# A decoder layer on one core: moving tiles at another residue of 512 bytes, and a re-ordered opening of the FFN

## The chip, the cores and the metric

The kernel runs on one core of a Trainium2 chip. The metric is the device time of one execution in microseconds (us); lower is better. The engines are named as in the profile: PE is the matrix engine (PEld its weight loads), DVE the vector engine, ACT the scalar engine, POOL the general-purpose one, SP the queue that issues most transfers.

## The reference

One layer of a hybrid decoder, 512 tokens by 1024 features, fp32, depth 1. Two token mixers read the same input projection; their outputs are gated, merged and projected; then comes a SwiGLU channel mixer (FFN) with 2816 hidden features.

```python
proj = h @ w_in                        # q_a k_a v_a r_a d_low q_b k_b v_b g_a g_b
y_a = (norm(gla(q_a, k_a, v_a, decay(d_low))) * silu(r_a)) @ w_branch_a
y_b = swa(rope(q_b), rope(k_b), v_b, sinks) @ w_branch_b
mix = (sigmoid(g_a) * y_a + sigmoid(g_b) * y_b) @ w_out
h = layer_norm(alpha * h + mix, ln1_g, ln1_b)
ffn = (silu(h @ w_gate) * (h @ w_up)) @ w_down
h = layer_norm(alpha * h + ffn, ln2_g, ln2_b)
```

## The kernel before

**Products.** Every operand of a large product is split into a high part, rounded to fp32r (`ACT.copy`, the tiles `..h`), and a low part, the remainder (a DVE subtraction, the tiles `..l`); a product is the three matmuls high·high, low·high, high·low. A matmul streams its *moving* operand, 128 partitions by 512 or 256 columns of 4 bytes, past a *stationary* operand of 128x128 that a weight load has put into the array. In the profile `pga<-xh,wh` reads: into `pga`, moving `xh`, stationary `wh`. There are two families. In `feat_tile` (L239) activations move and weights stand still: `pq`, `pka`, `pqa`, `pr`, `pgb`, `pga` stream x (`xh`, `xl`), `pbb` and `pba` stream the two mixers' outputs. In `pva` (L435), in the output projection `pw` (L793 and L802) and in the down projection `pdn` (L1059) weights move and activations stand still.

**Stages in order of time.** Input projection with both mixers woven into it; `pbb`, `pga`, `pba`; the output projection, columns 0 to 511 first (`pw0` to `pw3`, L793), then columns 512 to 1023 one token tile at a time (`out_half`, `pw1_0` to `pw1_3`, L802); LayerNorm and the FFN's first operands; the FFN's gate and up products; the down projection in two column halves (`pdn0`, `pdn1`); the last LayerNorm.

**The FFN** is a Strassen-Winograd scheme: for each of 11 column groups `i` the 2x2 block product is made of seven products (`seventh`, L918, 256 columns each) of sums of weight quarters (`b11`, `b12`, `b22`, `b21`; the sums `t1` = b11+b12, `t2` = b11+b22, `t3` = b12+b22, `t4` = b11+b21, each a DVE addition of 128x1024 in place, `weight_sum`, L896) with sums of activation quarters (`A11`, `A12`, `A22`, `S1` to `S4`). `prep_quarters(n)` makes sure that the first n weight operands are split (`whb`/`wlb` from plain quarters, `wht`/`wlt` from sums; L905 on ACT, L906 on DVE). `A11` and `A12` come from the normalised rows: for token tile t the sum `res` (`norm_part`, L739: one DVE scalar_tensor_tensor on the PSUM tile, then bn_stats), the statistics' root (`ya`, `wa`), the normalisation of both halves on ACT (L753), four transposes for each half on PE (`pt_h`, L823), the affine step on ACT (`h`, L841), and the split (`a`, L830/L831).

**Order and memory.** The program is written stage by stage, and a scheduler sets the order of instructions on each engine from its own estimates; `tc.issue_after(ins)` makes it place what is inside behind `ins`. Tiles come from pools; the left stack of pools (weights, scratch, late tiles, FFN tiles) and the right one (x parts, merged activations, sums) grow toward each other, and a tile's address is fixed by what was allocated before it. Three small fillers shift whole stacks: `LEVEL` (left), `EDGE` (right), `BESIDE` (between FFN operands). So a residue of a tile's address modulo 512 bytes is the same for a whole family. `piece(j, k)` makes the down projection's stationary operand `op` from the activation `act`, from a ring of n buffers.

Of the kernel before, what the change touches and what calls it, by code (L numbers as in the profile page):

```python
# [9 lines left out]
F32 = mybir.dt.float32  # L10
# [3 lines left out]
ALU = mybir.AluOpType  # L14
AX = mybir.AxisListType

P = 128
# [10 lines left out]
ALPHA = 2.0 ** 0.25  # L28
# [4 lines left out]

LEVEL, EDGE, BESIDE = 32, 24, 16

C_QA, C_KA, C_VA, C_RA, C_DL = 0, 512, 1024, 2048, 3072
C_QB, C_KB, C_GA, C_GB = 3088, 4112, 4368, 5392
# [3 lines left out]
def tile_decoder_layer(  # L43
# [23 lines left out]
    PE, ACT, DVE, POOL = nc.tensor, nc.scalar, nc.vector, nc.gpsimd  # L67

    const = ctx.enter_context(tc.tile_pool(name="const", bufs=1))
    small = ctx.enter_context(tc.tile_pool(name="small", bufs=6))  # L70
    level = ctx.enter_context(tc.tile_pool(name="level", bufs=1))
    level.tile([P, LEVEL], F32, tag="level", name="level")
    wpool = ctx.enter_context(tc.tile_pool(name="weights", bufs=1))
    psum = ctx.enter_context(tc.tile_pool(name="psum", bufs=4, space=bass.MemoryType.PSUM))

# [7 lines left out]
    right = phase("xparts", "right")  # L83
# [652 lines left out]
    def norm_part(ps, t, i, stats, slot, c0=0, c1=512, first=True):  # L736
        r = res[t][i][:, c0:c1]
        if first:
            DVE.scalar_tensor_tensor(r, r, ALPHA, ps[:, c0:c1], ALU.mult, ALU.add)  # L739
        else:  # L740
            DVE.tensor_tensor(r, r, ps[:, c0:c1], ALU.add)
        DVE.bn_stats(stats[:, slot, :], r)

    def norm_rows(t, stats, name):
        mv = stat(f"mv{name}{t}", 2)
# [50 lines left out]
    def out_half(t):  # L796
        ps = ps_mm(f"pw1_{t}")
        ts = slice(t * P, (t + 1) * P)
        n = 0
        for k in range(NK):  # L800
            for d, w in ((mh, wo[k][0]), (ml, wo[k][0]), (mh, wo[k][1])):
                PE.matmul(ps, d[k][:, ts], w, start=n == 0, stop=n == 3 * NK - 1)  # L802
                n += 1
        norm_part(ps, t, 1, st1[t], 1)

# [90 lines left out]
    def prep_quarters(count):  # L898
        while len(parts_) < min(count, len(flow)):
            j = len(parts_)  # L900
            i, q = flow[j]
            weight_sum(i, q)
            src = raw_pair(i)[SUMS[q][0] if q in SUMS else q]
            wh, wl = [wpool.tile([P, 1024], F32R, tag=t, name=f"{t}{q}{i}", bufs=5) for t in ("wh", "wl")]
            ACT.copy(wh, src)  # L905
            lows.append(DVE.tensor_tensor(wl, src, wh.bitcast(F32), ALU.subtract))  # L906
            parts_.append((wh, wl))
            if i > 1 and j + 1 < len(flow) and flow[j + 1][0] == i:
                weight_sum(*flow[j + 1])
            if q == "t1" and 0 < i < HF - 1:  # L910
                raw_pair(i + 1)
# [65 lines left out]
            acts[h, i] = act_tile(h, i)  # L977
            DVE.tensor_tensor(acts[h, i], g, u, ALU.mult)

    prep_quarters(4)  # L980
    for t in range(NT):
        norm_part(pw[t], t, 0, st1[t], 0)
    for i in (0, 1):
        weight_sum(i, "t1")
    for t in range(NT):
        out_half(t)
        norm_rows(t, st1[t][:, 0:2, :], "a")
        if 1 <= t <= 2:
            first_tokens(t - 1)
    right.release()  # L990
    right = phase("sums", "right")
    A22, S4 = [operand(right, n) for n in ("a22", "s4")]
    right.tile([P, BESIDE], F32, tag="beside", name="beside2")
    right2 = phase("sums2", "right")
    S1, S2, S3 = [operand(right2, n) for n in ("s1", "s2", "s3")]
    h22, s1, s3 = plain("h22"), plain("s1f"), plain("s3f")
# [29 lines left out]

    def piece(j, k):
        if (j, k) not in pieces:
            home, n = (tail, 8) if j else (right2, 6)
            op = home.tile([P, 2, T], F32R, tag="op", name=f"op{j}_{k}", bufs=n)  # L1030
            if not pieces:
                right2.tile([P, BESIDE], F32, tag="beside", name="beside3")
            src = acts[k // HF, k % HF]
            ACT.copy(op[:, 0], src)  # L1034
            DVE.tensor_tensor(op[:, 1], src, op[:, 0].bitcast(F32), ALU.subtract)  # L1035
            pieces[j, k] = op
        return pieces[j, k]
# [92 lines left out]
```

## Time and profile before

| what | value |
|---|---|
| time, three runs | 865.37, 869.77, 870.14 us (median 869.77) |
| the profiled execution | 870.17 us, of which the span from first to last instruction is 868.2 us |
| mean granted PE clock | 0.995 |
| PE / DVE / ACT / POOL busy | 97% / 67% / 46% / 11% of the span |
| transfers | 83.13 MB, mean 96 GB/s |

The profile is one execution. "Mean of one" in a group of matmuls is the modelled length of one matmul, which overlaps its neighbours; what a matmul takes in a stream is the spacing of starts, which is the length of a stretch in which PE never pauses, divided by the number of matmuls that start in it (a window's count also includes those that reach in over an edge).

### The profile page before, as it was taken

The numbers are of one execution on the slowest core, as the hardware profiler recorded it, in microseconds if no ns is written. First come the engines' busy times: TensorE is split into PE (matmuls) and PEld (weight loads), VectorE is DVE, ScalarE is ACT, GpSimd is POOL, SyncE is SP. The second block draws the span as 40 slices with busy tenths as digits, with TensorE's granted clock in tenths as the row PEclk, the third lists the DMA queues.
The fourth block names the chain that finished last, engine by engine and source line by source line (L and its number), as shares of the span: only waits on it lengthen the run. The fifth ranks groups of instructions, "written<-read, shape, count | busy, mean of one in ns | idle before, by whom it ended". The sixth has DMA issues, their size and how long they took to land.

```text
span 868.2 us, 12541 instructions
## 1 busy us (share of the span) xinstructions
PE 841.2 (97%) x4922; PEld 726.7 (84%) x4922; DVE 578.0 (67%) x997; ACT 401.2 (46%) x699; POOL 94.5 (11%) x102
## 2 busy tenths in 40 slices
PE   7999999999999999999999898999999999999995
PEld 7887777787888788888888788999999999888884
DVE  4898888586675623322444669987878786964447
ACT  4557565564453422122233295554545455642321
POOL 4240220021320131000123000000000000000001
PEclk9999999999999999999999999999999999999998
DMA  8423113113113223333328301244333326242202
GB/s 243 145 74 95 52 49 98 49 49 98 49 49 97 73 74 97 97 97 97 97 97 263 101 1 46 77 143 130 113 102 99 97 73 209 84 145 92 79 1 97
DMA packets 92683, 83.13 MB, mean 96 GB/s; under 512 B 4833, under 2 KB 79601, under 8 KB 92625
## 3 DMA queue, kind: packets, MB, share of 16 engines
q1 hardware_dynamic: 90480, 76.89, 29.2%
q0 software_dynamic: 1568, 4.41, 1.6%
q10 hardware_dynamic: 576, 1.05, 0.3%
q8 instruction: 38, 0.62, 0.3%
q14 instruction: 21, 0.16, 0.1%
HBM read 80.24 MB, written 2.10 MB: 95 GB/s over the span
## 4 chain that ended last, share of the span: by engine, by line
PE 91%; DVE 3%; SPq 2%; DMA 1%; issue 1%; ACT 1%; POOL 0%; POOLq 0%; DVEq 0%; ACTq 0%
PE pdn L1059 13%; PE fx L918 13%; PE fy L918 7%; PE pva L435 5%; PE pgb L239 5%; PE pq L239 5%; PE pga L239 5%; PE pr L239 5%; PE pbb L239 5%; PE pba L239 5%; PE fz L918 4%; PE pka L239 3%; PE pqa L239 3%; PE pw L802 3%; PE po L416 2%; PE pp L405 2%
## 5 line engine op out<-in xcount | busy, mean ns | idle before, releaser
L171 DVE TENSOR_TENSOR wl<-raw,wh 128x1024 fp32r<-128x1024 f32 x96 | 121.3, 1265 | 111.7 <-ACT wh L170 111.5
L170 ACT CAST wh<-raw 128x1024 fp32r<-128x1024 f32 x96 | 100.5, 1050 | 133.5 <-PE pdn L1059 34.3
L1059 PE MATMUL pdn<-wh,op 128*128 128x512 f32 (+1 forms) x396 | 110.7, 366 | 0.0
L1059 PEld LDWEIGHTS pdn<-wh,op 128*128 128x128 f32 x396 | 71.4, 189 | 12.2
L905 ACT CAST wht<-b 128x1024 fp32r<-128x1024 f32 x44 | 46.2, 1049 | 63.9 <-DVE b L896 52.9
L1059 PE MATMUL pdn<-wl,op 128*128 128x512 f32 (+1 forms) x198 | 72.0, 365 | 0.0
L918 PE MATMUL fx<-s,wht 128*128 128x256 f32 x352 | 63.4, 280 | 1.4 <-ACT wht L905 1.4
L906 DVE TENSOR_TENSOR wlt<-b,wht 128x1024 fp32r<-128x1024 f32 x44 | 53.7, 1222 | 9.9 <-ACT wht L905 9.9
L896 DVE TENSOR_TENSOR b<-b,b 128x1024 f32<-128x1024 f32 x44 | 53.5, 1220 | 5.2 <-DMA b<-in_w_ffn_up_dram 4.8
L918 PEld LDWEIGHTS fx<-s,wht 128*128 128x128 f32 x352 | 53.7, 188 | 1.8 <-ACT wht L905 1.8
L906 DVE TENSOR_TENSOR wlb<-b,whb 128x1024 fp32r<-128x1024 f32 x33 | 40.2, 1221 | 21.5 <-ACT whb L905 18.5
L918 PE MATMUL fx<-s,wlt 128*128 128x256 f32 x176 | 49.3, 281 | 1.9 <-DVE wlt L906 1.9
L905 ACT CAST whb<-b 128x1024 fp32r<-128x1024 f32 x33 | 34.5, 1050 | 31.5 <-PE fx L918 15.6
L1059 PEld LDWEIGHTS pdn<-wl,op 128*128 128x128 f32 x198 | 37.3, 188 | 6.1
L1034 ACT CAST op<-act 128x512 fp32r<-128x512 f32 x44 | 26.1, 618 | 22.4 <-PE pdn L1059 21.6
L918 PEld LDWEIGHTS fx<-s,wlt 128*128 128x128 f32 x176 | 32.9, 187 | 2.5 <-DVE wlt L906 2.3
L1035 DVE TENSOR_TENSOR op<-act,op 128x512 fp32r<-128x512 f32 x44 | 29.0, 687 | 8.8 <-ACT op L1034 8.8
L391 ACT ACTIVATE S<-S,nm 128x256 f32<-128x256 f32 (+1 forms) x64 | 30.1, 476 | 10.3 <-DVE es L388 6.1
L918 PE MATMUL fx<-a,whb 128*128 128x256 f32 x176 | 32.9, 281 | 1.8 <-ACT a L830 1.0
L918 PE MATMUL fy<-s,whb 128*128 128x256 f32 x176 | 33.1, 280 | 0.3 <-DVE s L831 0.3
L918 PE MATMUL fx<-a,wht 128*128 128x256 f32 x176 | 31.8, 280 | 0.5 <-DVE c L966 0.5
L918 PE MATMUL fy<-s,wht 128*128 128x256 f32 x176 | 32.1, 279 | 0.0
(445 smaller groups left out, 2269.4 us busy)
## 6 DMA issues: line engine op xcount, KB each, us to landing
raw<-in_w_in_dram SPq DMA_DIRECT2D x50, 512.0 KB, 3.6
b<-in_w_ffn_gate_dram SPq DMA_DIRECT2D x44, 256.0 KB, 4.0
b<-in_w_ffn_up_dram SPq DMA_DIRECT2D x44, 256.0 KB, 4.4
raw<-in_w_ffn_down_dram SPq DMA_DIRECT2D x22, 512.0 KB, 3.5
raw<-in_w_branch_b_dram SPq DMA_DIRECT2D x8, 512.0 KB, 3.3
raw<-in_w_branch_a_dram SPq DMA_DIRECT2D x8, 512.0 KB, 3.4
raw<-in_w_out_dram SPq DMA_DIRECT2D x8, 512.0 KB, 3.5
x<-in_x_dram SPq DMA_DIRECT2D x8, 256.0 KB, 6.3
```

Of the source, the lines that this page charges most:

```text
L170: ACT.copy(wh, raw)
L171: DVE.tensor_tensor(wl, raw, wh.bitcast(F32), ALU.subtract)
L239: PE.matmul(ps[:, n0:n1], w, d[k][:, n0:n1] if isinstance(d, list) else d[:, k, n0:n1], start=i == 0, stop=i == 3 * NK - 1)
L391: ACT.activation(S[h], S[h], AF.Exp, bias=nm[:, h : h + 1], accum_out=den[:, h : h + 1])
L435: PE.matmul(pa[c], d[:, k, cs], w, start=k == 0 and i == 0, stop=k == NK - 1 and i == 2)
L896: DVE.tensor_tensor(a, a, b, ALU.add)
L905: ACT.copy(wh, src)
L906: lows.append(DVE.tensor_tensor(wl, src, wh.bitcast(F32), ALU.subtract))
L918: PE.matmul(ps[:, n * HT : (n + 1) * HT], w[x][:, c0 : c0 + P], op[:, y, k, :], start=start and n == 0 and i == 0, stop=stop and n == 1 an ...
L1034: ACT.copy(op[:, 0], src)
L1035: DVE.tensor_tensor(op[:, 1], src, op[:, 0].bitcast(F32), ALU.subtract)
L1059: PE.matmul(ps[:, c0:c1], op[:, x, ts], w[y][:, c0:c1], start=start and n == 0, stop=stop and n == 2)
```

## The change

Three things are done.

1. *Placement.* The filler `LEVEL` of 32 floats is gone, which moves the whole left stack from residue 0 to 384 of 512 bytes; `BESIDE` grows from 16 to 48 floats, which puts the FFN's left operands back to 64; the right filler becomes `ROW - BESIDE` = 80 floats, which moves the FFN's right operands from 320 to 64. Worked out from the pools' sizes, the residues (moving, stationary) are:

| products | columns | matmuls | before | after |
|---|---|---|---|---|
| pq, pka, pqa, pr, pgb, pga | 512 | 960 | (384, 0) | (384, 384) |
| pva, pw | 512 | 384 | (0, 384) | (384, 384) |
| pbb, pba | 512 | 384 | (0, 0) | (384, 384) |
| pdn | 512 (132 more of 256) | 462 | (0, 256), later (0, 0) | (384, 384) |
| pk, pv, pd | 256 | 128 | (384, 0) | (384, 384) |
| FFN with A11, A12 moving | 256 | 528 | (64, 0) | (64, 384) |
| FFN with A22, S1 to S4 moving | 256 | 1320 | (320, 0) | (64, 384) |

2. *The FFN's opening.* The four additions on `pw0` to `pw3` come first, and `prep_quarters` behind the last of them; the sums `t1` and `t3` of the first two column groups are queued behind the residual additions of token tiles 1 and 2.
3. *The ring* of `op` buffers in the first half of the down projection has 5 instead of 6.

```diff
--- before.py
+++ after.py
@@ -33,7 +33,7 @@
 
 
 
-LEVEL, EDGE, BESIDE = 32, 24, 16
+EDGE, BESIDE, ROW = 24, 48, 128
 
 C_QA, C_KA, C_VA, C_RA, C_DL = 0, 512, 1024, 2048, 3072
 C_QB, C_KB, C_GA, C_GB = 3088, 4112, 4368, 5392
@@ -68,8 +68,6 @@
 
     const = ctx.enter_context(tc.tile_pool(name="const", bufs=1))
     small = ctx.enter_context(tc.tile_pool(name="small", bufs=6))
-    level = ctx.enter_context(tc.tile_pool(name="level", bufs=1))
-    level.tile([P, LEVEL], F32, tag="level", name="level")
     wpool = ctx.enter_context(tc.tile_pool(name="weights", bufs=1))
     psum = ctx.enter_context(tc.tile_pool(name="psum", bufs=4, space=bass.MemoryType.PSUM))
 
@@ -736,10 +734,11 @@
     def norm_part(ps, t, i, stats, slot, c0=0, c1=512, first=True):
         r = res[t][i][:, c0:c1]
         if first:
-            DVE.scalar_tensor_tensor(r, r, ALPHA, ps[:, c0:c1], ALU.mult, ALU.add)
+            done = DVE.scalar_tensor_tensor(r, r, ALPHA, ps[:, c0:c1], ALU.mult, ALU.add)
         else:
-            DVE.tensor_tensor(r, r, ps[:, c0:c1], ALU.add)
+            done = DVE.tensor_tensor(r, r, ps[:, c0:c1], ALU.add)
         DVE.bn_stats(stats[:, slot, :], r)
+        return done
 
     def norm_rows(t, stats, name):
         mv = stat(f"mv{name}{t}", 2)
@@ -801,7 +800,7 @@
             for d, w in ((mh, wo[k][0]), (ml, wo[k][0]), (mh, wo[k][1])):
                 PE.matmul(ps, d[k][:, ts], w, start=n == 0, stop=n == 3 * NK - 1)
                 n += 1
-        norm_part(ps, t, 1, st1[t], 1)
+        return norm_part(ps, t, 1, st1[t], 1)
 
 
 
@@ -977,20 +976,25 @@
             acts[h, i] = act_tile(h, i)
             DVE.tensor_tensor(acts[h, i], g, u, ALU.mult)
 
-    prep_quarters(4)
     for t in range(NT):
-        norm_part(pw[t], t, 0, st1[t], 0)
-    for i in (0, 1):
-        weight_sum(i, "t1")
+        urgent = norm_part(pw[t], t, 0, st1[t], 0)
+    with tc.issue_after(urgent.ins):
+        prep_quarters(2)
     for t in range(NT):
-        out_half(t)
+        urgent = out_half(t)
         norm_rows(t, st1[t][:, 0:2, :], "a")
+        with tc.issue_after(urgent.ins):
+            if t == 0:
+                prep_quarters(4)
+            elif t < 3:
+                for i in (0, 1):
+                    weight_sum(i, ("t1", "t3")[t - 1])
         if 1 <= t <= 2:
             first_tokens(t - 1)
     right.release()
     right = phase("sums", "right")
     A22, S4 = [operand(right, n) for n in ("a22", "s4")]
-    right.tile([P, BESIDE], F32, tag="beside", name="beside2")
+    right.tile([P, ROW - BESIDE], F32, tag="beside", name="beside2")
     right2 = phase("sums2", "right")
     S1, S2, S3 = [operand(right2, n) for n in ("s1", "s2", "s3")]
     h22, s1, s3 = plain("h22"), plain("s1f"), plain("s3f")
@@ -1026,7 +1030,7 @@
 
     def piece(j, k):
         if (j, k) not in pieces:
-            home, n = (tail, 8) if j else (right2, 6)
+            home, n = (tail, 8) if j else (right2, 5)
             op = home.tile([P, 2, T], F32R, tag="op", name=f"op{j}_{k}", bufs=n)
             if not pieces:
                 right2.tile([P, BESIDE], F32, tag="beside", name="beside3")
```

The same instructions run on each engine; what moves is shown at three places.

DVE at the end of the output projection's first half, before (`b11_0 <- b11_0, b12_0` is the sum t1 of group 0; `wlb110` the low part of quarter b11 of group 0; `res0_0 <- res0_0, pw0` the addition of token tile 0):

```order
L171 TENSOR_TENSOR wl73_4274<-raw73_4219,wh73_4273 128x1024
L906 TENSOR_TENSOR wlb110_4295<-b11_0_4282,whb110_4294 128x1024
L896 TENSOR_TENSOR b11_0_4282<-b11_0_4282,b12_0_4285 128x1024
L906 TENSOR_TENSOR wlb111_4311<-b11_1_4298,whb111_4310 128x1024
L906 TENSOR_TENSOR wlb210_4315<-b21_0_4291,whb210_4314 128x1024
L896 TENSOR_TENSOR b11_1_4298<-b11_1_4298,b12_1_4301 128x1024
L739 SCALAR_TENSOR_TENSOR res0_0_4128<-res0_0_4128,pw0_4151 128x512
L739 SCALAR_TENSOR_TENSOR res1_0_4130<-res1_0_4130,pw1_4152 128x512
L742 BN_STATS bna0_4147<-res0_0_4128 128x6
L739 SCALAR_TENSOR_TENSOR res2_0_4132<-res2_0_4132,pw2_4153 128x512
L742 BN_STATS bna1_4148<-res1_0_4130 128x6
```

and after:

```order
L169 TENSOR_TENSOR wl73_4270<-raw73_4215,wh73_4269 128x1024
L737 SCALAR_TENSOR_TENSOR res0_0_4124<-res0_0_4124,pw0_4147 128x512
L737 SCALAR_TENSOR_TENSOR res1_0_4126<-res1_0_4126,pw1_4148 128x512
L740 BN_STATS bna0_4143<-res0_0_4124 128x6
L737 SCALAR_TENSOR_TENSOR res2_0_4128<-res2_0_4128,pw2_4149 128x512
L740 BN_STATS bna1_4144<-res1_0_4126 128x6
L737 SCALAR_TENSOR_TENSOR res3_0_4130<-res3_0_4130,pw3_4150 128x512
L905 TENSOR_TENSOR wlb110_4299<-b11_0_4286,whb110_4298 128x1024
L740 BN_STATS bna2_4145<-res2_0_4128 128x6
L905 TENSOR_TENSOR wlb111_4315<-b11_1_4302,whb111_4314 128x1024
L740 BN_STATS bna3_4146<-res3_0_4130 128x6
```

Three splits and two sums stood ahead of the first addition; now the additions stand first, and the sums are gone from here (they come behind the additions on `pw1_1` and `pw1_2`).

ACT between the end of the output projection and the FFN's first product, before (`pt_h0_0` is the transposed first half of token tile 0, `pt_h1_0` that of tile 1, `wht10` the high part of sum t1 of group 0):

```order
L748 ACTIVATE ya1_4402<-mva1_4400,eps_104 128x1
L753 ACTIVATE res1_1_4131<-res1_1_4131,wa1_4404,ya1_4402 128x512
L753 ACTIVATE res1_0_4130<-res1_0_4130,wa1_4404,ya1_4402 128x512
L841 ACTIVATE h11_4280<-pt_h0_0_4414,lncol1_109,lncol0_108 128x128 x4
L841 ACTIVATE h12_4281<-pt_h0_1_4425,lncol1_109,lncol0_108 128x128 x4
L830 CAST a11_4278<-h11_4280 128x4x128
L905 CAST wht10_4635<-b11_0_4282 128x1024
L830 CAST a12_4279<-h12_4281 128x4x128
L748 ACTIVATE ya2_4465<-mva2_4463,eps_104 128x1
L841 ACTIVATE h11_4280<-pt_h1_0_4477,lncol1_109,lncol0_108 128x128 x4
L841 ACTIVATE h12_4281<-pt_h1_1_4488,lncol1_109,lncol0_108 128x128 x4
L830 CAST a11_4278<-h11_4280 128x4x128
```

and after:

```order
L904 CAST wht10_4633<-b11_0_4286 128x1024
L840 ACTIVATE h11_4276<-pt_h0_0_4410,lncol1_105,lncol0_104 128x128 x4
L752 ACTIVATE res1_1_4127<-res1_1_4127,wa1_4398,ya1_4396 128x512
L752 ACTIVATE res1_0_4126<-res1_0_4126,wa1_4398,ya1_4396 128x512
L840 ACTIVATE h12_4277<-pt_h0_1_4421,lncol1_105,lncol0_104 128x128 x4
L829 CAST a11_4274<-h11_4276 128x4x128
L747 ACTIVATE ya2_4461<-mva2_4459,eps_100 128x1
L840 ACTIVATE h11_4276<-pt_h1_0_4475,lncol1_105,lncol0_104 128x128 x4
L840 ACTIVATE h12_4277<-pt_h1_1_4486,lncol1_105,lncol0_104 128x128 x4
L829 CAST a12_4275<-h12_4277 128x4x128
L747 ACTIVATE ya3_4526<-mva3_4524,eps_100 128x1
L829 CAST a11_4274<-h11_4276 128x4x128
```

The normalisation of token tile 1 (`res1_1`, `res1_0`) has moved from ahead of tile 0's affine step to a place between its two halves, and both `a12` and the second `a11` come behind tile 1's affine step. On PE the transposes `pt_h0` stand in `pw1_2` before:

```order
L802 MATMUL pw1_2_4436<-wl72_4246,mh5_4045 128x512
L802 MATMUL pw1_2_4436<-wh73_4273,mh6_4088 128x512
L823 MATMUL pt_h0_0_4414<-ident_84,res0_0_4128 128x128 x4
L823 MATMUL pt_h0_1_4425<-ident_84,res0_1_4129 128x128 x4
L802 MATMUL pw1_2_4436<-wh73_4273,ml6_4089 128x512
L802 MATMUL pw1_2_4436<-wl73_4274,mh6_4088 128x512
```

and in the middle of `pw1_3` after, with `pt_h1` behind its last matmul:

```order
L801 MATMUL pw1_3_4497<-wl71_4212,mh3_3967 128x512
L822 MATMUL pt_h0_0_4410<-ident_80,res0_0_4124 128x128 x4
L822 MATMUL pt_h0_1_4421<-ident_80,res0_1_4125 128x128 x4
L801 MATMUL pw1_3_4497<-wh72_4241,mh4_4010 128x512
L801 MATMUL pw1_3_4497<-wh72_4241,ml4_4011 128x512
```

Tile 0's transposes have moved 17 matmuls back.

DVE where the down projection begins, before (`op0_k <- act, op0_k` is the low part of the operand for chunk k of the first half, `op1_k` of the second; `res <- res, g1` the scaling of the residual rows by the LayerNorm's gain):

```order
L1035 TENSOR_TENSOR op0_4_7248<-act0_4_5769,op0_4_7248 128x512
L1035 TENSOR_TENSOR op0_5_7264<-act0_4_5769,op0_5_7264 128x512
L978 TENSOR_TENSOR act1_10_7107<-c10_1_6923 128x512
L171 TENSOR_TENSOR wl78_7211<-raw78_7176,wh78_7210 128x1024
L978 TENSOR_TENSOR act1_10_7107<-c10_0_6922 128x512
L1035 TENSOR_TENSOR op1_0_7597<-act0_0_5040,op1_0_7597 128x512
L1035 TENSOR_TENSOR op1_1_7615<-act0_0_5040,op1_1_7615 128x512
L1035 TENSOR_TENSOR op1_2_7639<-act0_2_5305,op1_2_7639 128x512
L1035 TENSOR_TENSOR op1_3_7657<-act0_2_5305,op1_3_7657 128x512
L1035 TENSOR_TENSOR op1_4_7681<-act0_4_5769,op1_4_7681 128x512
L1035 TENSOR_TENSOR op1_5_7699<-act0_4_5769,op1_5_7699 128x512
L1068 TENSOR_TENSOR res0_0_4128<-res0_0_4128,g1_7140 128x512
```

and after:

```order
L1039 TENSOR_TENSOR op1_5_7695<-act0_4_5765,op1_5_7695 128x512
L1072 TENSOR_TENSOR res0_0_4124<-res0_0_4124,g1_7136 128x512
L1072 TENSOR_TENSOR res0_1_4125<-res0_1_4125,g1_7136 128x512
L1072 TENSOR_TENSOR res1_0_4126<-res1_0_4126,g1_7136 128x512
L1072 TENSOR_TENSOR res1_1_4127<-res1_1_4127,g1_7136 128x512
L1072 TENSOR_TENSOR res2_0_4128<-res2_0_4128,g1_7136 128x512
L1072 TENSOR_TENSOR res2_1_4129<-res2_1_4129,g1_7136 128x512
L1072 TENSOR_TENSOR res3_0_4130<-res3_0_4130,g1_7136 128x512
L1072 TENSOR_TENSOR res3_1_4131<-res3_1_4131,g1_7136 128x512
L1039 TENSOR_TENSOR op1_6_7719<-act0_6_6229,op1_6_7719 128x512
L1039 TENSOR_TENSOR op1_7_7737<-act0_6_6229,op1_7_7737 128x512
L1039 TENSOR_TENSOR op0_5_7260<-act0_4_5765,op0_5_7260 128x512
```

The low part of `op0_5` has moved from the second place of the one list to behind all eight scalings and two more splits; with five buffers it takes over that of `op0_0`.

## The prediction

> **What bounds the kernel now.** I read the page first: the busy shares, then the chain that ended last, by engine.
>
> ```profile
> span 868.2 us, 12541 instructions
> PE 841.2 (97%) x4922; PEld 726.7 (84%) x4922; DVE 578.0 (67%) x997; ACT 401.2 (46%) x699; POOL 94.5 (11%) x102
> PE 91%; DVE 3%; SPq 2%; DMA 1%; issue 1%; ACT 1%; POOL 0%; POOLq 0%; DVEq 0%; ACTq 0%
> ```
>
> PE is busy in 841 of 868 us and carries 91% of the chain. So the time is the sum of what PE's matmuls take in a stream plus 27 us in which PE has nothing to do. Each of the three edits has to be priced in one of these two currencies. Next I read PE's groups with shapes kept apart, columns: line, instruction, count, busy us, mean ns of one, idle before.
>
> ```profile
> L239 PE MATMUL pga<-xh,wh 128*128 128x512 f32 x64 | 25.3, 395 | 0.0
> L239 PE MATMUL pba<-oah,wh 128*128 128x512 f32 x64 | 24.9, 389 | 0.0
> L239 PE MATMUL pbb<-obh,wh 128*128 128x512 f32 x64 | 25.0, 391 | 0.0
> L435 PE MATMUL pva<-wh,xh 128*128 128x512 f32 x64 | 25.3, 398 | 0.0
> L793 PE MATMUL pw<-wh,mh 128*128 128x512 f32 x32 | 12.6, 395 | 0.0
> L1059 PE MATMUL pdn<-wh,op 128*128 128x512 f32 x308 | 95.0, 390 | 0.0
> L1059 PE MATMUL pdn<-wh,op 128*128 128x256 f32 x88 | 16.4, 282 | 0.0
> L918 PE MATMUL fx<-s,wht 128*128 128x256 f32 x352 | 63.4, 280 | 1.4 <-ACT wht L905 1.4
> L918 PE MATMUL fx<-a,wht 128*128 128x256 f32 x176 | 31.8, 280 | 0.5 <-DVE c L966 0.5
> L266 PE MATMUL pd<-xl,wd 128*128 128x256 f32 x16 | 3.9, 281 | 0.0
> ```
>
> Same shape, same clock, yet three families: products whose two operands have the same residue or differ by 256 bytes (pba, pbb, pdn) take 389 to 391 ns, and those whose residues differ by 128 modulo 256 (pga, pva, pw) take 395 to 398. The mean is a modelled length, so I check it against stretches in which PE never pauses (columns: window, its length, PE busy and count, clock, transfers).
>
> ```profile
> 326.35:369.98 43.63, 43.63 (x195) 1.00 0.33 96
> 369.98:414.77 44.79, 44.79 (x193) 1.00 0.31 94
> 414.77:458.31 43.54, 43.54 (x193) 1.00 0.30 97
> 600.00:640.00 40.00, 40.00 (x342) 1.00 0.37 106
> 852.10:857.50 5.40, 5.40 (x47) 1.00 0.25 97
> ```
>
> The first three are pbb, pga and pba, 192 matmuls each: 43.63/192 = 227.2 ns, 44.79/192 = 233.3 ns, 43.54/192 = 226.8 ns. So 6 ns hang on the residues, 2.6%. For 256 columns the fourth window (FFN) gives 40.00/340 = 117.6 ns at a difference of 64 or 320, and the last one (45 starts of pdn at equal residues) 5.40/45 = 120.0 ns.
>
> **The placement.** pva and pw move what pga holds still: weights at 0 stream past activations at 384, in pga x at 384 streams past weights at 0. Both are slow alike, 395 and 395 to 398, and pdn is fast at 256 against 0. An operand at 384 is thus no ailment of one side; the distance of the two, modulo 256, fits all six 512-column rows. After the change that distance is 0 in every one of them. Gain: pq 192, pka 96, pqa 96, pr 192, pgb 192, pga 192, pva 192, pw0 to pw3 96, together 1248 matmuls. Price of one: 395 minus 389.5 of the rows, 5.5 ns; by the windows 233.3 - 226.8 = 6.5. I take 5.5, because pga's window holds small pauses too: **-6.9 us**, bounds -8.1 (6.5 ns) and 0 (next rival). All these stages are PE-bound (the windows are 100% busy), so it counts in full. The 96 matmuls of `pw1` are in the opening's sum. pbb, pba and pdn keep a distance of 0 modulo 256 and cost nothing; pk, pv, pd go from 128 to 0, 128 matmuls of 256 columns between 281 and 282 ns by the rows: nothing.
>
> [...]
>
> For the FFN's 1848 matmuls the new distance is 192 modulo 256, which no row of before has. The nearest rows: 64 (280 ns, 117.6 in the stream), 128 (281, pd), 0 (282, 120.0). If the sign of the distance does not matter, as pga against pva suggests, 192 is 64 seen from the other side: 0. If it is like distance 0: 1848 x 2.4 ns = +4.4 us. Below nothing cannot be excluded, but the fastest row is already the one it comes from. I take **0**, range -1 to +4.4.
>
> **The opening.** DVE and PE there:
>
> ```profile
> 480.19 1.22 DVE L906 TENSOR_TENSOR wlb<-b,whb 128x1024 fp32r<-128x1024 f32 x1 [1.62 <-ACT whb L905]
> 481.33 1.22 DVE L896 TENSOR_TENSOR b<-b,b 128x1024 f32<-128x1024 f32 x1
> 482.47 1.28 DVE L739 SCALAR_TENSOR_TENSOR res<-res,pw 128x512 f32<-128x512 f32 x2
> 496.22 0.69 DVE L739 SCALAR_TENSOR_TENSOR res<-res,pw 128x512 f32<-128x512 f32 x1 [2.44 <-PE pw L802]
> ```
>
> ```profile
> 480.40 0.40 PE L793 MATMUL pw<-wl,mh 128*128 128x512 f32 x1
> 483.20 0.50 PE L802 MATMUL pw<-wh,mh 128*128 128x512 f32 x1 [2.41 <-DVE res L739]
> 483.20:487.20 4.00, 4.00 (x11) 0.57 0.29 87
> ```
>
> PE stood 2.4 us because `pw1_0` needs the PSUM tile of `pw0`, which DVE gave back only behind a split (480.19) and a sum (481.33). Then the clock was 0.57 on average for 4 us: 11 matmuls in 4.00 us where 11 x 0.233 = 2.56 were needed, 1.4 us lost. With the additions first, `pw0`'s is done (1.28 us for two) while PE still runs the last of `pw1` to `pw3`, so `pw1_0` starts at 480.63 on the old time axis: 2.6 + 1.4 = 4.0 us earlier. Who collects them? The FFN's start hangs on ACT:
>
> ```profile
> 499.39 1.52 ACT L753 ACTIVATE res<-res,wa,ya 128x512 f32<-128x512 f32 x2 [1.17 <-DVE wa L751]
> 505.29 0.66 ACT L830 CAST a<-h 128x512 fp32r<-128x512 f32 x1
> 505.81 0.34 ACT L748 ACTIVATE ya<-mva,eps 128x1 f32<-128x1 f32 x1
> 506.59 2.90 ACT L841 ACTIVATE h<-pt_h,lncol,lncol 128x128 f32<-128x128 f32 x8 [0.45 <-PE pt_h L823]
> 509.34 0.65 ACT L830 CAST a<-h 128x512 fp32r<-128x512 f32 x1
> 505.95 1.03 PE L823 MATMUL pt_h<-ident,res 128*128 128x128 f32 x8
> 510.05 0.50 PE L918 MATMUL fx<-a,whb 128*128 128x256 f32 x2 [0.96 <-ACT a L830]
> ```
>
> Now `pt_h0` stands behind 84 of `pw1`'s 96 matmuls: 480.63 + 84 x 0.2268 = 499.7. ACT begins 0.64 later (505.95 to 506.59) and has in its new order a half of tile 0 (1.45, half of 2.90), the normalisation of tile 1 (1.52), the other half (1.45), a11 (0.66), a root (0.34), both halves of tile 1 (2.90), a12 (0.66), a root (0.34), a11 (0.65): 9.97 us, less about 0.14 of overlap at each of 9 hand-overs (505.29 to 505.81 is 0.52 for a row of 0.66), 8.7. The first FFN product can start at 499.7 + 0.64 + 8.7 + 0.1 = 509.1, against 510.05: the 4 us shrink to 0.9, because PE now waits for `a` from the end of `pt_h1` (480.63 + 96 x 0.2268 + two blocks of transposes of 0.8 = 504.0) some 5 us instead of 0.96. Behind `fx0` stands `pt_h2`, whose normalisation on ACT comes only after this chain as before, so I count half, -0.4. A wait of 2.4 us cost 1.4 us of clock behind it; one of 5 us should cost at least that: +1.4 to +1.7 (3.4 us at half speed). [...]
>
> The sums `t3` come back further on, where DVE is the bound:
>
> ```profile
> 535.21 3.49 DVE L896 TENSOR_TENSOR b<-b,b 128x1024 f32<-128x1024 f32 x3
> 528.00:547.00 19.00, 14.81 (x114) 13.47 (x112) 18.61 (x17) 12.52 (x15) 0.00 (x0) 1.00 0.30 85
> ```
>
> DVE works 18.6 of 19.0 us there and PE only 14.8. Two of these sums leave (3.49 for three, 1.13 each from start to start): -2.3 us. They now run beside `pw1_2`/`pw1_3`, where DVE has room (it idled 2.44 us ahead of the addition at 496.22). Opening in all: -0.4 + 1.7 - 2.3 = **-1.0 us**; bounds -4.3 (no clock loss, front gain 0.9 counted, some 1 us more of that stretch) and +1.5 (the sums' room in the stretch is eaten by the waits that follow).
>
> **The ring of five.** Before, PE never paused as the down projection began:
>
> ```profile
> 742.77 3.69 DVE L1035 TENSOR_TENSOR op<-act,op 128x512 fp32r<-128x512 f32 x6
> 746.38 4.90 DVE L1068 TENSOR_TENSOR res<-res,g 128x512 f32<-128x512 f32 x8
> 754.21 1.22 DVE L171 TENSOR_TENSOR wl<-raw,wh 128x1024 fp32r<-128x1024 f32 x1
> 737.02:797.00 59.98, 59.98 (x268) 1.00 0.34 114
> ```
>
> Now `op0_5` takes `op0_0`'s place, so its cast waits for the end of chunk 0 (737.02 + 12 x 0.227 = 739.7, early enough), but its low part stands on DVE behind the eight scalings, `op1_6` and `op1_7`. DVE is one op0 part shorter ahead of it: the scalings start at 745.8 to 746.1, end 4.84 later, three splits of 0.60 follow: 752.7. PE needs chunk 5 at 737.02 + 60 x 0.227 = 750.6 and has four matmuls without the low part: 751.5. Wait 1.2 to 1.3 us. `op0_6` then stands behind two scalings, `wl79` (1.2) and one more: 752.7 + 1.2 + 1.2 + 0.6 + 0.6 = 756.3, where PE comes to it at 752.8 + 12 x 0.227 = 755.5: 0.8 to 0.9. **+2.1 us**; bounds 0 (the gain's transfer or ACT lets DVE come earlier) and +3.8 (PE's clock drops behind the two waits, as at the opening).
>
> **Sum.** -6.9 + 0 - 1.0 + 2.1 = -5.8 us, 870.17 to 864.4 for the profiled execution. That one lay 0.4 above the median of 869.77; the three runs spread by 4.8. Forecast **864.0 us**. I call under 0.5% (4.35 us) no change; a measurement of this kernel tells no less.
>
> **Rivals.**
> *Distance 192 is slow (15%).* FFN at 120.0 ns: +4.4, so -1.4 us: 868.4. For it: only 2% separate the three known distances; against: mirror image of the fastest.
> *The residues are not the cause (18%).* Then pga is slow for another reason, perhaps what is written to SBUF beside it, and the placement brings 0; left are -1.0 and +2.1, 870.9. [...] Against it: pga, pba and pbb alternate within 132 us at the same clock and the same transfers (94 to 97 GB/s).
> *A residue of 384 is itself slow (14%), the other side.* If an operand at 384 costs 5.5 ns whichever it is, pga and pva stay as slow as they are (one such operand before, two now), while pbb 192, pba 192 and pdn 462 become slow: 846 x 5.5 = +4.7, 132 more of pdn and the FFN's stationary operand at nothing known. With -1.0 + 2.1 that is +5.8: 875.6; if two such operands add up, 1248 x 5.5 = 6.9 more. It decides from the point where pba's mean exceeds 393. For it: every slow 512-column row has one operand at 384; against: the FFN's moving tiles lie at 64 and 320, off any 128 boundary, and have the shortest rows of their shape.
>
> **Chances.** The forecast, 49%, with a range of its own of 860 to 866.5: faster 45, same 4. Slow 192: same 13, faster 2. No cause: same 15, slower 3. Slow 384: slower 14. The rest (an opening that loses more than 3 us), 4: same 3, slower 1. Together faster 47, same 35, slower 18. The range runs from the forecast with the low ends of placement and opening to the rival without a cause: 859 to 872.
>
> **What would show it.** Right: the mean of pga, pva and pw falls to 389 to 391 and pba, pbb, pdn stay; no PE wait on `res` at `pw1_0`; a wait of PE on `a` of some 5 us and a clock dip behind it; two PE waits on `op` near the start of the down projection; FFN rows at 280. Wrong: pba at 395 (slow 384), pga unmoved (no cause), FFN rows at 282 or more, or `fx0` starting earlier than 28.5 us after `pw1_0`.

## The result, and the profile after

The changed kernel took 860.31 us (median of 11 runs, 859.15 to 868.29) against 870.75 us before (11 runs, 865.37 to 873.06): a ratio of 0.9896, 95% interval 0.9868 to 0.9923, 10.4 us less. The forecast was 864.0, range 859 to 872, and "faster" as the likeliest sign. The time lies inside the range, but the gain is nearly twice the 5.8 us that the sum gave, and one term of the sum accounts for that.

The profiled execution was one of the two longer ones of the eleven (867.15 us; the nine others lie at 859.15 to 860.56). The same kernel was profiled once more (`after_again`), in an execution of 861.25 us, like the majority. The span cut into four stages shows where both stand (columns: window in us, length, PE busy and count, clock, transfers; the edges are the first matmuls of `pq`, `pw0`, `fx0`, `pdn0` and the last of `pdn`). Before:

```profile
27.94:458.31 430.37, 427.52 (x2098) 1.00 0.27 79
458.31:510.05 51.74, 48.37 (x210) 0.97 0.48 153
510.05:737.02 226.97, 221.74 (x1865) 1.00 0.35 103
737.02:858.01 120.99, 120.99 (x596) 1.00 0.24 83
```

After, first profile:

```profile
28.69:454.44 425.75, 422.90 (x2098) 1.00 0.27 80
454.44:504.93 50.49, 45.50 (x210) 0.99 0.53 156
504.93:731.78 226.85, 223.14 (x1864) 0.99 0.36 103
731.78:854.82 123.04, 121.58 (x596) 1.00 0.24 82
```

After, second profile:

```profile
30.20:455.82 425.62, 422.78 (x2098) 1.00 0.27 80
455.82:506.32 50.50, 45.50 (x209) 0.98 0.52 156
506.32:725.93 219.61, 215.77 (x1865) 0.99 0.37 106
725.93:848.92 122.99, 121.60 (x596) 1.00 0.24 82
```

| stage | forecast | first profile | second profile |
|---|---|---|---|
| pq to pw0 (placement) | -6.3 | -4.6 | -4.8 |
| pw0 to fx0 (pw0 -0.5, opening -0.4) | -0.9 | -1.3 | -1.2 |
| fx0 to pdn0 (clock +1.7, sums -2.3, distance 0) | -0.6 | -0.1 | **-7.4** |
| down projection (ring) | +2.1 | +2.1 | +2.0 |

The two profiles of one kernel differ in the FFN alone. The rows of the page by shape answer to those of before: the 512-column products that stood at 395 to 398 ns went down.

```profile
L237 PE MATMUL pga<-xh,wh 128*128 128x512 f32 x64 | 24.9, 389 | 0.0
L237 PE MATMUL pba<-oah,wh 128*128 128x512 f32 x64 | 24.9, 389 | 0.0
L433 PE MATMUL pva<-wh,xh 128*128 128x512 f32 x64 | 25.2, 396 | 0.0
L792 PE MATMUL pw<-wh,mh 128*128 128x512 f32 x32 | 12.4, 389 | 0.0
L237 PE MATMUL pr<-xl,wh 128*128 128x512 f32 x64 | 25.3, 396 | 0.0
```

pga and pw are now equal to pba, as forecast. The products that are woven with the mixers' work fell less than pga's 6 ns: on the mean of their three rows pr by 2, pva by 3, the others by 4 to 5. Weighted with their counts, the seven products of the first stage give 4.6 us by these rows, which is why the stage gives 4.7 and not 6.3. The waits of PE (columns: total us, times, longest) and the windows around the opening and the down projection's start:

```profile
PE fx L917 <- ACT a L829: 5.0, 1, 5.0
PE pdn L1063 <- DVE op L1039: 1.5, 2, 0.9
499.80:504.93 5.13, 0.14 (x3) 0.88 0.00 0
504.93:510.51 5.58, 5.58 (x25) 0.50 0.00 0
747.40 0.50 PE L1063 MATMUL pdn<-wh,op 128*128 128x512 f32 x1 [0.93 <-DVE op L1039]
750.94 0.50 PE L1063 MATMUL pdn<-wh,op 128*128 128x512 f32 x1 [0.53 <-DVE op L1039]
```

The wait on `res` is gone, PE waits 5.0 us for `a` in its place, and the two waits on `op` are there. The clock was at half from 503.68 to 510.51; 5.6 us of that lie behind `fx0`.

### The profile page after: what moved, and what is told of

Its sections match the earlier page's. It is cut to its first block, busy times and chain, and to the rows that moved or that the text cites. A ratio compares the mean times of both kernels' runs of the same rounds, so it can differ in the third digit from the quotient of the medians.

```text
span 865.1 us, 12541 instructions
## 1 busy us (share of the span) xinstructions
PE 834.8 (96%) x4922; PEld 725.2 (84%) x4922; DVE 577.3 (67%) x997; ACT 401.1 (46%) x699; POOL 94.4 (11%) x102
## 4 chain that ended last, share of the span: by engine, by line
PE 91%; DVE 4%; ACT 2%; DMA 1%; issue 1%; POOL 0%; SPq 0%; POOLq 0%; ACTq 0%
PE fx L917 13%; PE pdn L1063 11%; PE fy L917 7%; PE pva L433 5%; PE pq L237 5%; PE pr L237 5%; PE pgb L237 5%; PE pbb L237 5%; PE pba L237 5%; PE pga L237 5%; PE fz L917 4%; PE pka L237 3%; PE pqa L237 3%; PE pw L792 3%; PE pw L801 2%; PE po L414 2%
## 5 line engine op out<-in xcount | busy, mean ns | idle before, releaser
L917 PE MATMUL fx<-a,whb 128*128 128x256 f32 x176 | 34.9, 294 | 5.8 <-ACT a L829 5.0
L1038 ACT CAST op<-act 128x512 fp32r<-128x512 f32 x44 | 26.1, 618 | 25.2 <-PE pdn L1063 24.5
L917 PEld LDWEIGHTS fx<-a,whb 128*128 128x128 f32 x176 | 28.9, 200 | 6.3 <-ACT a L829 5.2
```

What stands on the lines that cost most here:

```text
L917: PE.matmul(ps[:, n * HT : (n + 1) * HT], w[x][:, c0 : c0 + P], op[:, y, k, :], start=start and n == 0 and i == 0, stop=stop and n == 1 an ...
```

## The experiments

**The placement alone** has the order of instructions of before on every engine, and a ring of six. Smaller fillers keep the FFN at a distance of +64, as before.

```diff
-    ffn.tile([P, BESIDE], ...)        +    ffn.tile([P, 16], ...)
-    right.tile([P, ROW - BESIDE], ..) +    right.tile([P, 48], ...)
-    right2.tile([P, BESIDE], ...)     +    right2.tile([P, 16], ...)
     (opening and ring of 6 as before)
```

> The placement alone: residues as after the change for every 512-column product (distance 0 modulo 256), FFN at a distance of 64 as before, six op buffers, and on every engine the order of instructions of before. Theory A (the distance of the two operands modulo 256 sets the spacing of 512-column matmuls): pga, pq, pva and pw fall to 389 to 391 ns, pbb, pba, pdn stay, the opening's wait of PE on res (2.4 us) and its half clock stay; 5.5 to 7 us faster than before. If the measured surplus of the whole change (10.4 us in the medians where the sum said 5.8) belongs to the placement, 10 to 12 us faster. Rival B (the residues are not the cause): within 1 us of before.

869.14 us, ratio 0.9981 (0.9956 to 1.0007). In this series the executions of before form two groups, six of 31 at 864.2 to 865.2 us and the others at 869.0 to 873.0 (median 871.7); against this upper group the placement alone, whose ten executions form one group (median 869.1), is 2.6 us faster. That is less than theory A asked for and more than rival B. The spacing did what the theory says, pga at 389 ns, and the first stage took 425.63 us (29.80 to 455.43), 4.7 less. But:

```profile
455.43:508.69 53.26, 47.41 (x210) 0.97 0.49 148
PE pw L801 <- DVE res L737: 4.9, 1, 4.9
```

The stage from `pw0` to `fx0` grew from 51.74 to 53.26 us, because PE's wait on `res` grew from 2.4 to 4.9 us: of 4.7 us, 1.5 are lost there. (The execution's start, which lies between 27.9 and 30.2 us in these traces, hid 1.9 more in this profile.)

It is tempting to say that PE, coming earlier, only waits longer for a split that keeps its time. The later traces speak against it: `d64` and `map2` (below) have the same opening and a first stage as long as before's (430.6 and 430.9 us), and still wait 4.7 and 3.5 us. What differs is how fast the FFN's weight quarters arrive. They are asked for 3.2 us after the start of `pw0` in each of these traces, and the conversion ahead of the last split waits for one of them. That conversion, in before, in the placement alone and in `d64`, starts 20.8, 22.7 and 22.7 us after `pw0`:

```profile
479.11 1.05 ACT L905 CAST whb<-b 128x1024 fp32r<-128x1024 f32 x1 [1.80 <-DMA b<-in_w_ffn_up_dram]
478.14 1.04 ACT L904 CAST whb<-b 128x1024 fp32r<-128x1024 f32 x1 [2.40 <-DMA b<-in_w_ffn_up_dram]
482.51 1.04 ACT L906 CAST whb<-b 128x1024 fp32r<-128x1024 f32 x1 [2.49 <-DMA b<-in_w_ffn_up_dram]
```

The stretch from 16 to 24 us after `pw0`, in before, in the opening alone (addresses of before), in the placement alone and in `d64` (last column: GB/s):

```profile
474.31:482.31 8.00, 6.49 (x28) 1.00 1.12 327
476.41:484.41 8.00, 8.00 (x36) 1.00 1.08 316
471.43:479.43 8.00, 5.92 (x27) 1.00 1.04 283
475.77:483.77 8.00, 6.13 (x27) 1.00 1.17 290
```

The two traces with the left stack at residue 0 moved 327 and 316 GB/s there, the twelve with it at 384, 416 or 448 moved 282 to 291, whichever opening they have. So the placement seems to slow these transfers, and with the old opening PE pays for it. Why they are slower was not tested.

**The opening alone**: addresses and ring of before, the changed opening.

> The opening alone: residues and ring of before, the additions first and the sums t1 and t3 behind the residual additions. Theory A: fx0 starts 28 to 30 us after pw1_0, PE waits some 5 us for a with a half-clock stretch behind it, the two sums leave the DVE-bound stretch; 0 to 2 us faster than before. Rival C (the opening is where the surplus came from): 4 to 6 us faster.

870.91 us, ratio 1.0007 (0.9977 to 1.0037). PE's wait for `a` is 5.0 us and `fx0` starts 511.94 - 482.72 = 29.2 us after `pw1_0`, both as forecast; the stage took 51.53 us (0.2 less) and the FFN 227.46 (0.5 more). So the opening by itself is worth next to nothing. Its use is that PE no longer waits for the quarters' splits there, so that the placement's gain comes through: together they took 5.9 us out of the first two stages, where the placement alone kept 3.2. The times agree: in the upper groups of this series the placement alone is 2.6 us under before, the opening alone 0.7, both together with a ring of six (next run) 6.3.

**The ring of six** on top of the change, with the FFN at +64 to make room:

> The changed kernel with six op buffers again, made to fit by smaller fillers (FFN at a distance of 64, op at 128 against 384, a distance of 256, so 0 modulo 256). Theory A: the two PE waits on op (0.9 and 0.6 us in the profile after) go, pdn at 389 to 391 ns; 2 us faster than the changed kernel. If the distance counts modulo 512 and not 256, pdn rises to 395 or so and it is 1 to 2 us slower.

865.24 us, ratio to before 0.994 (0.991 to 0.9971). The waits on `op` are gone and the down projection took 120.99 us again (732.18 to 853.17), so a distance of 256 counts as 0 here: 2.1 us, the size that the forecast gave the ring. Against the changed kernel's median it is slower all the same; the FFN's distance, which had to change to make room, turned out to be the reason (below).

**A later place for the sums** (`best`): as `ring6`, with

```diff
-        urgent = out_half(t)
-        norm_rows(t, st1[t][:, 0:2, :], "a")
+        out_half(t)
+        urgent = norm_rows(t, st1[t][:, 0:2, :], "a")   # returns the step that makes wa
```

> As ring6, and the sums and quarters queued behind the last statistics step (wa) of a token tile instead of behind its residual addition. PE's transposes pt_h0 then stand in pw1_2 again. Theory A: fx0 starts 25 to 26 us after pw1_0, PE's wait for a falls from 5 us to under 2, no half clock behind it; 4 us faster than ring6 and 6 faster than the changed kernel. Rival D (the FFN takes the gain back in the DVE-bound stretch behind it): within 1 us of ring6.

861.37 us, ratio 0.9909 (0.9874 to 0.9945). `pw0` to `fx0` took 46.71 us (454.67 to 501.38) where the change takes 50.49, the first 3.8 us of the opening that really are saved; PE's clock there stayed at 1.00. The FFN behind it took 227.12 us (501.38 to 728.50), 0.9 more than `ring6`'s 226.22, so a part is taken back there; the median still fell by 3.9 against `ring6`, as theory A said, and rival D is out. Against the changed kernel, where 6 us were expected, it is 1 us slower; the reason follows.

**The changed kernel again**, because its eleven runs fell into two groups and mostly into the lower one, unlike every other kernel's:

> The changed kernel once more, beside the same runs of before. In every series so far each kernel has two groups of times some 6 us apart (before 864.2 to 865.2 and 869.0 to 873.1), the changed kernel 9 of 11 times in its lower group, all others 1 in 5 to 10. Theory E (the groups have nothing to do with the change): most runs lie at 866 to 868, the lower group is as rare as for the others, and within one group the change is worth 3.5 to 5 us. Rival F (the change itself brings the kernel into the lower group): again most runs at 859 to 861, 10 us faster.

859.71 us, four executions of four at 858.5 to 861.3, ratio 0.9876 (0.9834 to 0.9917). Theory E fell: the lower group belongs to the change. The second profile says where it lies. From the last pause of PE in the FFN's first groups to the next pause, some 185 us later, 1578 matmuls follow each other; the same stretch before, after (first and second profile):

```profile
547.52:733.26 185.74, 185.74 (x1579) 1.00 0.38 111
542.38:728.11 185.73, 185.73 (x1578) 1.00 0.39 111
543.42:722.17 178.75, 178.75 (x1579) 1.00 0.40 115
```

185.74/1577 = 117.8 ns a matmul in the first two, 178.75/1577 = 113.3 ns in the third: 7.0 us, with the same instructions, clock and addresses as in the second. Nothing lies between: in the traces with the FFN at a distance of +64 or -64 each such stretch has one of the two paces from end to end, but for up to four matmuls at its start.

**Two maps of distances**, order and ring of before. `d64` puts the weights at 448, `map2` at 416:

```diff
+    level.tile([P, 16], ...)          # d64; map2: 8
-    ffn.tile([P, BESIDE], ...)        # d64: none; map2: 24
-    right.tile([P, ROW - BESIDE],..)  # d64: 80; map2: 16
-    right2.tile([P, BESIDE], ...)     # d64: none; map2: 16
```

> A map of distances, order and ring of before: weights at 448. L239's products get a distance of -64 (384 against 448), pva and pw +64, pbb and pba 0, the first half of the down projection 128 (448 against 64), its second half 0; in the FFN the products with A11 and A12 moving get 0 (448, 448), the others 128 (64 against 448). Theory A (distance modulo 256): pdn's first half rises from 226.7 to 232 ns a matmul, pbb and pba stay at 226.7; FFN 120 ns with A11 and A12, about 118.7 with the others; the value of +64 and -64 for 512 columns is open, 226 to 233, the same for both signs. Rival G (a residue of 384 of one operand is what is slow): pdn's first half stays at 226.7, L239's products at 232, pva and pw at 232.

> A second map, order and ring of before: weights at 416. 512 columns: L239 at -32, pva and pw at +32, the first half of the down projection at -96 modulo 256 (416 against 256), pbb and pba at 0. 256 columns: A11 and A12 moving at +96 (0 against 416, modulo 256), the others at -96. If the sign counts as at 64: for 512 columns L239 slower than pva and pw; for 256 columns the -96 products quicker than the +96 ones. Theory A as first put (sign without effect): L239 equals pva and pw, and all FFN products are alike.

One execution each, 876.81 and 876.92 us. `pga`, `pba`, the first 240 matmuls of the down projection, and 40 us of the FFN, in `d64`:

```profile
371.43:416.23 44.80, 44.80 (x194) 1.00 0.31 94
416.23:459.77 43.54, 43.54 (x194) 1.00 0.29 97
742.11:797.88 55.77, 55.77 (x243) 1.00 0.34 113
600.00:640.00 40.00, 40.00 (x339) 1.00 0.39 106
```

and in `map2`:

```profile
371.68:416.48 44.80, 44.80 (x194) 1.00 0.31 94
416.48:460.03 43.55, 43.55 (x193) 1.00 0.29 97
741.73:797.95 56.22, 56.22 (x243) 1.00 0.34 113
600.00:640.00 40.00, 40.00 (x339) 1.00 0.36 106
```

For 512 columns (moving minus stationary, modulo 256): distance 0 takes 43.54/192 = 226.8 ns, -64 and -32 both 44.80/192 = 233.3, 128 55.77/240 = 232.4, and -96 56.22/240 = 234.3. The means by shape of `pw` at +64 and +32 are 392 and 395 against 389 at 0. pba is as quick at 448 and at 416 (43.54 and 43.55 us) as at 0 or 384 (43.54 and 43.52): at these four the residue itself made no difference, the distance did, and rival G is out. But the sign made a difference too: at -64 pga has a mean of 394 ns, where `pw` at +64, at 392, lies between (at 32 the rows of pga and `pw`, 396 and 395, are nearly alike). The forecast's "mirror" is therefore wrong for 512 columns. For 256 columns, distances of 0, 128, 96 and -96 make the FFN slower: 40 us hold 339 matmuls, against 342 at +64 in the prediction's row. At -64 there is a sign of the quick pace outside the FFN as well: in `d64` the rows `xh,wl` of pk and pv, 256 columns at -64, have a mean of 276 ns, where they have 281 to 283 at 128 (before) and at 0 (placement alone).

**Both stacks moved by 64 bytes:**

```diff
-    edge.tile([P, EDGE], ...)         +    edge.tile([P, 8], ...)
+    level.tile([P, 16], ...)
     (fillers and opening as in the placement alone)
```

> As the placement alone, but both stacks moved by 64 bytes: 512-column products all at 448 against 448, the down projection's first half 448 against 192 (a distance of 256), the FFN at a distance of 64 or -192 as there. Theory A (only the distance counts): pga, pba, pbb, pdn at 226.7 ns a matmul as in the placement alone. Rival G (the residues themselves count): one of them departs from 226.7 by over 2 ns.

One execution, 867.9 us: pga 43.52 us for its 192, pba 43.52, the down projection's first 240 54.43 (226.8 ns), with 448 against 448 and 448 against 192. Theory A holds in this point.

**The sign in the FFN alone** (`neg64`): the placement alone with the fillers 48, 16, 48 in place of 16, 48, 16, which makes +64 into -64.

```diff
-    ffn.tile([P, 16], ...)            +    ffn.tile([P, 48], ...)
-    right.tile([P, 48], ...)          +    right.tile([P, 16], ...)
-    right2.tile([P, 16], ...)         +    right2.tile([P, 48], ...)
```

> The placement alone with one thing different: the fillers put the FFN's moving tiles at a distance of -64 (64 and 320 against 384) where the placement alone had +64. Order of instructions and ring of before. The traces so far show two paces of the FFN stream, 117.8 ns a matmul (before and all kernels at +64) and 113.3 ns (the changed kernel, at -64, in its lower group). Theory H (the sign of the distance sets the pace): FFN at 113.3 ns in most runs, 6 to 8 us faster than the placement alone (869.1), 861 to 863. Rival I (the changed opening, with the half clock at the FFN's start, puts the stream into the quicker pace): FFN stays at 117.8, the time at 867 to 870.

862.17 us, ratio 0.9922 (0.9892 to 0.9951), with four executions at 859.9 to 862.2 and three at 866.7 to 868.1. The profiled one:

```profile
545.47:724.53 179.06, 179.06 (x1581) 1.00 0.40 114
```

113.3 ns. The order of instructions is that of before, so rival I (the opening sets the pace) is out, and the distance it is; but it does not decide alone, since three executions of seven were, by their times, at the slow pace. (Of ten executions of before in the same series none was in the lower group.)

**The best parts together**: `best2` is `best` at -64 (fillers as in `neg64`); `best3` is the changed kernel with only the later place for the sums; `best4` is `best3` with six `op` buffers, which fit when `beside3` goes.

```diff
  (best2, best3, best4 against the changed kernel)
-        urgent = out_half(t)
+        urgent = norm_rows(...)       # all three
-    right.tile([P, ROW - BESIDE],..)  # best2: 16
-    home, n = ... (right2, 5)
+    home, n = ... (right2, 6)         # best2, best4
-    right2.tile([P, BESIDE], ...)     # best4
```

> As best, with the FFN at a distance of -64 as in neg64. Theory H: FFN at 113.3 ns, 853 to 856, some 7 us under best and 4 to 6 under the changed kernel. Rival I: as best, 861.

> The changed kernel with one difference: sums and quarters stand behind the last statistics step of a token tile (wa) instead of behind its residual addition. All addresses and the ring of five as in the change. Theory J (the FFN's pace is drawn anew at each pause of PE and kept to the next; at -64 it falls on 113.3 ns in about 2 of 3 draws, at +64 in 1 of 8): fx0 starts 25 us after pw1_0 instead of 28.7; two groups of times, 855 to 857 in most executions and 862 to 864 in the others; both paces appear in one trace. Rival L (what counts is the distance modulo 512: 192, as in the changed kernel, nearly always gives 113.3, where the 448 of most FFN products in neg64 and best2 gives it in half of them): nearly all executions at 855 to 857.

> As best3 with six op buffers, which fit when the filler ahead of them goes; op then lies at 64, a distance of +64 to the weights that move past it, where the map gave 229 ns for 512 columns. The two PE waits on op (1.5 us) go, 264 matmuls of the first half become 2.3 ns longer (+0.6 us): 1 to 2 us under best3 in either group of times.

| kernel | FFN distance | median us | ratio to before | executions in the lower group |
|---|---|---|---|---|
| best2 | -64 | 861.08 | 0.9865 (0.9815 to 0.9915) | 1 of 4 (853.6) |
| best3 | -64 | 857.14 | 0.9843 (0.9824 to 0.9861) | 5 of 5 |
| best4 | -64 | 858.17 | 0.9853 (0.9818 to 0.9887) | 3 of 6 (854.2 to 854.9) |

`best2`'s median is the 861 of rival I and not theory H's 853 to 856: three of its four executions were, by their times, at the slow pace. The profiles of `best2` and `best3` hold the long stretch at one pace each, and that of `best3` the whole opening:

```profile
538.47:724.20 185.73, 185.73 (x1578) 1.00 0.39 110
539.69:718.44 178.75, 178.75 (x1578) 1.00 0.40 114
455.42:502.36 46.94, 45.49 (x209) 1.00 0.58 168
```

`best2`'s stretches before the long one were at 113.3, 113.5, 117.6, 114.0 and 117.7 ns: both paces in one execution, with a pause of PE between any two. Counting every stretch of ten or more matmuls between pauses in the FFN, in the twelve traces at +64 or -64, by its median spacing (113 ns as quick, 117 to 118 as slow): 32 of 44 are quick at -64, 3 of 46 at +64. Counting executions: 26 of 37 in the lower group at -64 (`after`, `after_again`, `neg64`, `best2`, `best3`, `best4`), 12 of 111 at +64 (before, `place_only`, `open_only`, `ring6`, `best`). So the distance shifts the odds, and a new pace can begin at each pause, as theory J has it. But the odds are not the same at every pause: at -64 the stretches of 97 and of 21 matmuls were quick in all twelve cases, the first stretch of 23 in two of six.

Theory J also expected two groups for `best3`, and rival L one; all five executions lie at 856.0 to 859.4, as rival L has it. `best4`, with the same distances in the FFN, then gave both groups, three of six each, against "nearly always quick at 192". Modulo 512 the quick kernels have 192 in the FFN throughout in `after`, `best3` and `best4` (21 of 26 executions), and 448 for most products in `neg64` and `best2` (5 of 11). The two at 448 ran on one chip, on which before had none of ten executions in its lower group (nine of 61 in the other series), so this comparison is not clean, and rival L stays open in a weaker form.

In `best3`, `fx0` started 502.36 - 477.18 = 25.2 us after `pw1_0`, as expected. In `best4` the waits on `op` are gone, and the first 240 matmuls of its down projection, at +64, took 228.9 ns each, as expected. Its lower group (854.2 to 854.9) is the lowest with more than one execution; by medians `best3` is the quickest. Within the quick pace `best3` lies some 2.5 us under the changed kernel and `best4` some 5.

## Why the prediction was right, and where it was not

- *Placement, -6.9.* Mechanism right: in `shift64` and `d64`, whose weights both lie at 448, pga takes 226.7 ns at a distance of 0 and 233.3 at -64. Why a distance costs time, no run here shows. Size: pq to `pw0` -4.7 instead of -6.3. The term was mis-sized in the six products woven with the mixers' small matmuls, whose rows fell by 2 to 5 ns, where pga's 395 to 389 was applied to all 1248. The reason for taking 5.5 and not 6.5, small pauses in pga's window, doesn't hold: the starts there lie 224 to 238 ns apart throughout.
- *"All these stages are PE-bound, so it counts in full."* This held only with the changed opening. Alone, the placement lost 1.5 of its 4.7 us at the wait on `res`, where the weight quarters came 1.9 us later after `pw0`; the sum had no term for slower transfers, nor for the opening taking PE off that wait.
- *FFN at the new distance, 0, range -1 to +4.4.* This is the step that failed. "If the sign of the distance does not matter, 192 is 64 seen from the other side" was taken from pga against pva, both at 128, where plus and minus are the same distance: they could not show a sign. And "the fastest row is already the one it comes from" took 117.8 for a floor; the trace of before itself had one stretch of 23 matmuls whose starts lie 22 x 113.3 ns apart:

```profile
529.89:532.38 2.49, 2.49 (x23) 1.00 0.02 7
```

  Measured: -7.0 us in the long stretch, by the times in 13 of 15 executions of the changed kernel, and 0 in the other two. Without it the change is worth 3 to 4 us. That the time lies inside the range is luck in this term: the range's low end was added up from placement and opening, not from a quicker FFN, and the forecast of 864.0 lies between the two groups, at a time that none of the 15 executions had. What decides the pace at a pause stays open.
- *Opening, -1.0.* The chain was right: `fx0` 504.93 - 476.20 = 28.7 us after `pw1_0` (forecast 28.5), wait 5.0 (some 5), half clock behind it. `pw0` to `fx0` gave -1.3 against -0.9. The clock term was too small for this kernel: 3.4 us at half speed were counted (what the clock of 0.57 over 4.00 us in before comes to), 5.6 us stood behind `fx0` (5.9 in `open_only`, 3.1 in `ring6`, whose FFN was 1.2 us shorter than `open_only`'s). The +1.7 and -2.3 behind `fx0` can't be read apart: `best`, with no half clock there, still took 227.1 us. The opening alone was worth 0.0 +/- 0.3%, inside its bounds.
- *Ring, +2.1.* Measured +2.0 to +2.1 and gone with six buffers. The profile's two waits, 0.93 and 0.53 us, count only from the modelled end of the matmul before. Counted by starts, 746.08 to 747.40 and 750.03 to 750.94, and with one matmul of 0.34 us behind each, the two pauses cost 1.20 and 0.80 us more than a stream of 0.227 us a matmul: the 1.2 and 0.8 that were worked out.
- *Rivals.* Slow residue of 384: out (pba 389 ns at 384, 416 and 448). No cause: out (pga). Slow 192: out, and with its sign turned.

## What to carry to other kernels

Where matmuls of one shape show different means, sort them by where their two operands lie relative to each other (here 226.8 against 233.3 ns for 512 columns) before looking for waits; but measure the distance that the new layout will have, plus and minus apart: here the three distances of before did not give the fourth (113.3 ns at -64, 117.8 at +64). A gain in one stage need not reach the end if the next place that PE waits at stays (here 3.2 of 4.7 us were kept): ask what that wait hangs on, and look at it in a kernel that has the wait without the gain before blaming the gain. A filler that moves operands moves the destinations of transfers too, so compare their GB/s (here 316 and 327 with the stack at residue 0, 282 to 291 elsewhere). And when a kernel's times form two groups, profile an execution of each: here both groups had the same program, and one row told them apart.

## What had not been expected of the hardware

- A stream of 256-column matmuls, each with its weight load, whose operands lie 64 bytes apart modulo 256, keeps one of two paces from one pause to the next, 113.3 or 117.8 ns, over as many as 1578 matmuls. What decides at the pause is open; the sign of the distance shifts the odds (quick in 32 of 44 stretches at -64, in 3 of 46 at +64).
- Transfers of the FFN's weight quarters ran at 316 and 327 GB/s, 16 to 24 us after `pw0`, in the two traces with their stack at residue 0 of 512 bytes, and at 282 to 291 in the twelve with another residue. Whether the residue of the destination is the cause was not tested.
- A pause of PE of 2.4 us was followed by half clock (before: 0.57 on average over the next 4.00 us), and so was one of 1.46 us ahead of `fx0` in `best3`, while one of 1.45 us in `best2`, at the same place, was not. The two pauses, the half clock in `best3` and the same stretch in `best2`:

```profile
502.36 0.51 PE L918 MATMUL fx<-a,whb 128*128 128x256 f32 x2 [1.46 <-ACT a L830]
501.34 0.51 PE L918 MATMUL fx<-a,whb 128*128 128x256 f32 x2 [1.45 <-ACT a L830]
503.38:506.79 3.41, 3.03 (x15) 0.50 0.00 0
501.34:506.00 4.66, 3.56 (x25) 1.00 0.00 0
```
